# The fifth score products of two heads as 64-row products in opposite halves of the array, and score banks by head

## The chip, the core and the metric

The kernel runs as one program on one core of a Trainium2 chip. The metric is the device time of one execution in microseconds (us). The engines are named as in the profile: PE is the matrix engine (TensorE), PEld its weight loads, DVE is VectorE, ACT is ScalarE, POOL is GpSimd, SP is the engine that issues most of the DMAs. PSUM is the memory into which PE writes its sums; this kernel uses it in banks of 512 float32 values for each of 128 partitions.

## The reference

A trunk of two layers works on 256 positions of 2048 channels. Each layer normalises its input, projects it, sends one part through a causal convolution with layer norm and one part through latent attention with 16 heads, gates and adds both, projects the sum and adds it to the input. What the change touches are the scores of attention:

```python
q = jnp.concatenate([q[..., :QK_NOPE], rope(q[..., QK_NOPE:], cos, sin)], axis=-1)   # 128 + 64 values
k = jnp.concatenate([k[..., :QK_NOPE], rope(k[..., QK_NOPE:], cos, sin)], axis=-1)
...
s = jnp.einsum('bqhd,bkhd->bhqk', q_i, k, preferred_element_type=jnp.float32) * scale
mask = key_chunk[None, :] <= q_chunk[:, None]        # chunks of 64, blocks of 128 queries
p = jax.nn.softmax(jnp.where(mask, s, -jnp.inf), axis=-1)
```

So a head's query and key have 128 values without and 64 with rotation ("rotary"). The queries come in two blocks of 128. Block 0 sees the first 128 keys only, block 1 all 256.

## The kernel before

**Split numbers.** Every float32 operand of a product is split into a high part and a low part (a float32r value and the rest), and a product is formed as high·high + low·high + high·low. For the big projections ACT makes `hi` from the raw weights, DVE makes `lo`, and PE multiplies pieces of 2 × 128 rows of weights: 12 products of 512 columns for each piece, into the banks `acc`. The weights for `hi` are prepared three pieces ahead of PE, those for `lo` two.

**The order of the work.** A wrapper (`InOrder`, its recording line is L135, which is why every row of the profile names L135) keeps each engine's instructions in the order in which the code issues them. `background(n)`, called after each piece, advances a slot counter and issues the attention steps that fall due in that slot between the pieces of the projections; `late` steps come at the end of the same slot. For each pair of heads, eight pairs in a layer, the steps are: factors, scaling of keys, a turn through DRAM, splits, `scores` (17 slots after the pair's start, or up to 4 later), `maxima` right behind it, `exponentials` two slots later, and later the values.

**The operands of the scores.** `nope_t` holds the 128 plain values of the pair's queries and keys, high and low, with the 128 values on the array's rows. The 64 rotary values fill half of the rows: head 0 owns rows 0 to 63, head 1 rows 64 to 127 (`halves`). In `rope_t[:, 0, h]`, the rotary queries, the head's own half holds the high part and the other half the low part; in `rope_t[:, 1, h]`, the keys, both halves hold the high part. `rope_l[:, h]` has the keys' low part in the own half and zeros in the other.

**`scores` (L835).** For each head three products make the scores of block 0, with high·high and low·high in the one half of the columns and high·low in the other. Five products of 256 columns each make the scores of block 1; the fifth is the rotary queries against `rope_l`, where the zeros cancel the other half. The sums stand in two banks: `s0` has block 0 of both heads, `s1` block 1 of both heads. That is 16 products for a pair.

**`maxima` (L859).** ACT copies one half of block 0's columns from PSUM to `sx`, DVE adds the other half, overwrites the masked corners of `sx` and of `s1`, and takes the negated maxima into `nb`. `exponentials` (L873) then reads `sx` and `s1`. At the very end of the program `products_at_end` (L303) uses the bank of `s0` for one last quarter of the output.

Of the kernel before, what the change touches and what calls it, by code (L numbers as in the profile page):

```python
# [11 lines left out]
F32 = mybir.dt.float32  # L12
# [7 lines left out]
P = 128  # L20
T = 2
SEQ = 256
# [101 lines left out]
def trunk(ctx: ExitStack, tc: tile.TileContext, xT, x, g_in, pos, win, wuq, wukv, wpc, wpm, wo, cst, rows, invf, out):  # L124
# [19 lines left out]
    pe, vec, act, gps, sp = (InOrder(e) for e in (nc.tensor, nc.vector, nc.scalar, nc.gpsimd, nc.sync))  # L144
# [16 lines left out]
    s_p = pool("s", 1, space=PSUM)  # L161
# [140 lines left out]

    def products_at_end(last, n, pts, stat, evacuate, evacuate_half):  # L303

        own = s_p.tile([P, n // 2], F32, tag="s0", name="right_half")

        def issue(t, places, out, columns=slice(0, n), start=False, stop=False):
            todo = [(j, kk, p) for j in places for p in range(3) for kk in range(KS)]
            for at, (j, kk, p) in enumerate(todo):
                hi, lo, _ = done[last[j]]  # L310
                sh, sl = stat(NCT - KS * len(last) + j * KS + kk, t)
                stationary, w = ((sh, hi), (sl, hi), (sh, lo))[p]
                pe.matmul(out, stationary, w[:, kk, columns], start=start and at == 0, stop=stop and at == len(todo) - 1)

        half = n // 2
        issue(0, (0, 1), pts[0][:, :n], stop=True)
        evacuate(0, pts[0][:, :n])
        issue(1, (0,), pts[1][:, :n])
        issue(1, (1,), pts[1][:, :half], slice(0, half), stop=True)
        evacuate_half(0, pts[1][:, :half], True)  # L320
        evacuate_half(half, pts[1][:, half:n], False)
        issue(1, (1,), own, slice(half, n), start=True, stop=True)
        evacuate_half(half, own, True)

    def product(planned, stat, evacuate, evac_at=EVAC_AT, costs=(0.0, 0.0), before=None, tardy=None, final=None):
# [8 lines left out]
        for j, i in enumerate(mine):  # L334
            for a in range(HI_AHEAD + 1):
                split_hi(i + a)
                if a <= LO_AHEAD:
                    split_lo(i + a)
            hi, lo, _ = done[i]
            if before:  # L340
                before(j)
            if final and j >= len(mine) - 2:
                if j == len(mine) - 1:
                    products_at_end(mine[-2:], n, pts, stat, evacuate, final)
                background(n)
                continue
            for t, kk, part in order_of_products(i, j == len(mine) - 1, j == tardy):
                k = j * KS + kk
                sh, sl = stat(k, t)
                stationary, w = ((sh, hi), (sl, hi), (sh, lo))[part]  # L350
                pe.matmul(
                    pts[t][:, :n], stationary, w[:, kk, :],
                    start=k == 0 and part == 0, stop=k == nk - 1 and part == 2,
                )
            if j == len(mine) - 1:
                steps.insert(0, (clock[0] + 1 + evac_at, costs, evac))
            background(n)
# [205 lines left out]
    for l in range(DEPTH):  # L563
# [101 lines left out]
        def pair_of(b, A=A):  # L665
            if b not in A.pairs:


                A.pairs[b] = dict(
                    qk=work2.tile([P, T, 4, 6, 32], F32, tag="qk", name="qk"),  # L670
                    vh=A.v_split[b % 3][0],
                    vl=A.v_split[b % 3][1],
                    ss=small.tile([P, 2, T, 2], F32, tag="ss_p", name="ss_p"),
                )
            return A.pairs[b]
# [87 lines left out]
        def attention(b, pair_of=pair_of, ss_d=ss_d, kpe=kpe, ccq=ccq, ssq_t=ssq_t, gqk=gqk, A=A):  # L763
            p, st = pair_of(b), {}
            nope_t, rope_t, rope_k, rope_l = A.nope_t, A.rope_t, A.rope_k, A.rope_l
# [35 lines left out]
            halves = (slice(0, ROPE), slice(ROPE, 2 * ROPE))  # L801
# [31 lines left out]
                at_slot(1, lambda: [vec.tensor_sub(lo, z, hi.bitcast(F32)) for lo, z, hi in subs], 1.8)  # L833

            def scores():  # L835
                s0 = s_p.tile([P, 2, 2, P], F32, tag="s0", name="s0")
                s1 = s_p.tile([P, 2, SEQ], F32, tag="s1", name="s1")

                for h in range(2):
                    qs = slice(0, P)  # L840
                    pe.matmul(s0[:, h], rope_t[:, 0, h, qs], rope_k[:, :, h, qs], start=True, stop=False)
                    pe.matmul(s0[:, h, 0, :], nope_t[:, 1, h, qs], nope_t[:, 2, h, qs], start=False, stop=False)
                    pe.matmul(s0[:, h], nope_t[:, 0, h, qs], nope_t[:, 2:4, h, qs], start=False, stop=True)
                for h in range(2):
                    qs = slice(P, SEQ)
                    terms = [
                        (rope_t[:, 0, h, qs], rope_t[:, 1, h, :]),
                        (nope_t[:, 0, h, qs], nope_t[:, 2, h, :]),
                        (nope_t[:, 0, h, qs], nope_t[:, 3, h, :]),
                        (nope_t[:, 1, h, qs], nope_t[:, 2, h, :]),  # L850
                        (rope_t[:, 0, h, qs], rope_l[:, h, :]),
                    ]
                    for n, (qa, ka) in enumerate(terms):
                        pe.matmul(s1[:, h, :], qa, ka, start=n == 0, stop=n == len(terms) - 1)
                st["s"] = s0, s1

                late.append(maxima)
# [66 lines left out]
            later(NOPE_AT, split_nope, 0.0, 1.8)  # L924
            later(ROPE_AT, split_rope, 0.0, 2.5)
            later(SCORES_AT, scores, 1.85, 0.35)
            later(EXP_AT, exponentials, 0.0, 3.3)
            later(P_BACK_AT, lambda: back_in("p"))
# [7 lines left out]
        s1 = layer_c.tile([P, 2, SEQ], F32, tag="s1c", name="s1c")  # L936
# [508 lines left out]
```

## Time and profile before

| | |
|---|---|
| time, median of 3 runs | 1876.08 us (1876.0 to 1877.35) |
| profiled execution, first to last instruction | 1875.0 us on core 0, granted TensorE clock 1.000 |
| what lies around the span, by the median | 1.1 us (the profiled execution's time as a whole is not listed) |
| PE, matmuls | 1869.4 us busy, 8577 products |
| DVE, ACT, POOL busy | 84%, 73%, 26% |
| the chain that ended last | PE 99%: `acc` 96%, `s` 2%, `o_ps` 1% |
| score products `s<-qk_t` | 224 of 256 columns, 32 of 128 columns, all of 128*128 |

A product's row on PE gives its start and a modelled end; products are pipelined, so the next one starts before the last one's row ends. What a product costs in a busy stretch is the distance between two starts. In a shape such as "128*128 128x256" the first two numbers are the rows and columns of the weights, the last is the product's columns. Two layers with eight pairs each make 16 calls of `scores`.

### The profile page before, as it was taken

What the parts mean: (1) busy time and instruction counts of PE and PEld (TensorE: products, weight loads), DVE (VectorE), ACT (ScalarE), POOL (GpSimd) and SP (SyncE); (2) the same over time, 40 slices, a digit from 0 to 9 for tenths busy, and PEclk for the clock granted to TensorE, in tenths of its full rate; (3) what the DMA queues carried; (4) which work ended last, traced back from release to release, by engine and by line L of the source; (5) the groups of instructions that cost most, each with busy time, mean ns of one, the idle gap of its engine ahead of it and who ended that gap; (6) DMA issues with size and microseconds to landing.
All of it is one profiled execution on the core that took longest, in us unless ns stands there. A gap on an engine that the chain in (4) does not pass through costs nothing.

```text
span 1875.0 us, 27166 instructions
## 1 busy us (share of the span) xinstructions
PE 1869.4 (100%) x8577; PEld 1570.9 (84%) x8577; DVE 1578.0 (84%) x2453; ACT 1360.5 (73%) x2510; POOL 495.7 (26%) x942
## 2 busy tenths in 40 slices
PE   9999999999999999999999999999999999999999
PEld 8988888888888888888899888888888888888887
DVE  6899998898999988766679899889899999885664
ACT  7678888888888876644557688788889888574442
POOL 1055555542200000122221455555322000001210
PEclk9999999999999999999999999999999999999999
DMA  9688878787765566678876787887877556667775
GB/s 322 219 264 255 261 256 258 257 275 226 244 204 192 194 207 218 208 239 278 290 234 216 260 267 253 260 255 262 267 231 242 196 191 204 206 206 222 239 250 166
DMA packets 138960, 445.05 MB, mean 237 GB/s; under 512 B 23680, under 2 KB 29312, under 8 KB 138816
## 3 DMA queue, kind: packets, MB, share of 16 engines
q1 hardware_dynamic: 105120, 359.89, 59.2%
q0 software_dynamic: 32832, 82.62, 13.8%
q8 instruction: 67, 1.10, 0.2%
q10 hardware_dynamic: 864, 0.80, 0.1%
q14 instruction: 77, 0.63, 0.1%
HBM read 399.18 MB, written 44.04 MB: 236 GB/s over the span
## 4 chain that ended last, share of the span: by engine, by line
PE 99%; DMA 1%; DVE 0%; ACT 0%; SPq 0%; issue 0%; DVEq 0%
PE acc L135 96%; PE s L135 2%; PE o_ps L135 1%; DMA raw<-in_win 0%; DMA gx<-in_g 0%; DVE xres L135 0%; ACT hi L135 0%; PE var L135 0%; PE mu L135 0%; SPq L135 0%; DVEq L135 0%
## 5 line engine op out<-in xcount | busy, mean ns | idle before, releaser
L135 ACT CAST hi<-raw 128x1024 fp32r<-128x1024 f32 (+3 forms) x682 | 700.3, 1033 | 405.0 <-PE acc L135 348.9
L135 DVE TENSOR_TENSOR lo<-raw,hi 128x1024 fp32r<-128x1024 f32 (+3 forms) x682 | 814.0, 1195 | 191.5 <-PE acc L135 145.7
L135 PE MATMUL acc<-hi,hT 128*128 128x512 f32 (+2 forms) x1728 | 419.6, 382 | 0.0
L135 PEld LDWEIGHTS acc<-hi,hT 128*128 128x128 f32 x1728 | 319.6, 188 | 59.1
L135 PE MATMUL acc<-hi,h_hi 128*128 128x512 f32 (+2 forms) x864 | 260.5, 383 | 1.3 <-ACT hi L135 1.3
L135 PE MATMUL acc<-hi,h_lo 128*128 128x512 f32 (+2 forms) x864 | 260.1, 382 | 0.0
L135 ACT ACTIVATE tap<-u_t,cst 128x256 f32<-128x256 f32 x542 | 235.7, 501 | 2.8 <-DVE v_t L135 2.8
L135 PE MATMUL acc<-lo,h_hi 128*128 128x512 f32 (+2 forms) x864 | 229.7, 382 | 0.0
L135 PE MATMUL acc<-lo,hT 128*128 128x512 f32 (+2 forms) x864 | 229.3, 382 | 0.0
L135 DVE TENSOR_TENSOR v_t<-v_t,tap 128x512 f32<-128x512 f32 x271 | 186.4, 688 | 9.7 <-DVE v_t L135 0.9
L135 POOL DMA_DIRECT2D turned<-turn_d x88 | 49.4, 562 | 531.0 <-DVE v_t L135 315.0
L135 PEld LDWEIGHTS acc<-hi,h_lo 128*128 128x128 f32 x864 | 161.0, 188 | 30.1
L135 PEld LDWEIGHTS acc<-hi,h_hi 128*128 128x128 f32 x864 | 160.0, 188 | 30.9 <-ACT hi L135 2.2
L135 PEld LDWEIGHTS acc<-lo,h_hi 128*128 128x128 f32 x864 | 160.5, 188 | 30.2 <-DVE lo L135 0.3
L135 PEld LDWEIGHTS acc<-lo,hT 128*128 128x128 f32 x864 | 160.6, 188 | 29.9
L135 DVE SCALAR_TENSOR_TENSOR v_t<-u_t,cst,v_t 128x256 f32<-128x256 f32 x418 | 178.4, 480 | 2.0
L135 POOL DMA_DIRECT2D turn_d<-gate x184 | 100.5, 554 | 290.6 <-DVE gate L135 177.6
L135 PE MATMUL acc<-hi,ycT 128*128 128x512 f32 x512 | 127.8, 389 | 0.0
L135 PE MATMUL acc<-hi,oT 128*128 128x512 f32 x512 | 127.7, 389 | 0.0
L135 PE MATMUL acc<-hi,yT 128*128 128x512 f32 x512 | 127.5, 388 | 0.0
L135 PE MATMUL acc<-hi,qkc 128*128 128x512 f32 x448 | 115.4, 389 | 0.0
L135 PEld LDWEIGHTS acc<-hi,ycT 128*128 128x128 f32 x512 | 96.1, 188 | 20.0
(176 smaller groups left out, 2227.1 us busy)
## 6 DMA issues: line engine op xcount, KB each, us to landing
raw<-in_win SPq DMA_DIRECT2D x382, 512.0 KB, 4.2
raw<-in_wpm SPq DMA_DIRECT2D x64, 512.0 KB, 3.3
raw<-in_wpc SPq DMA_DIRECT2D x64, 512.0 KB, 4.2
raw<-in_wo SPq DMA_DIRECT2D x64, 512.0 KB, 4.9
raw<-in_wukv SPq DMA_DIRECT2D x32, 512.0 KB, 4.1
turned<-turn_d POOLq DMA_DIRECT2D x56, 256.0 KB, 4.7
raw<-in_win SPq DMA_DIRECT2D x32, 384.0 KB, 4.6
raw<-in_wuq SPq DMA_DIRECT2D x24, 512.0 KB, 4.3
```

What stands on the lines that cost most here:

```text
L135: ins = getattr(self.engine, name)(*a, **k)
```

## The change

The fifth product of each head now takes only the 64 rows of the head's own half, for the queries as weights and for the keys, in place of 128 rows of which 64 met zeros. The two fifth products stand next to each other behind the other fourteen. A pair's scores stay 2 banks, but each bank now holds one head (block 0 in its first 256 columns, block 1 in its last 256), and both banks are one tile, `s`. `products_at_end` takes the same tile and uses the first 256 columns of it.

```diff
         def products_at_end(last, n, pts, stat, evacuate, evacuate_half):
 
-        own = s_p.tile([P, n // 2], F32, tag="s0", name="right_half")
+        own = s_p.tile([P, 2, 512], F32, tag="s", name="right_half")[:, 0, : n // 2]
...
             def scores():
-                s0 = s_p.tile([P, 2, 2, P], F32, tag="s0", name="s0")
-                s1 = s_p.tile([P, 2, SEQ], F32, tag="s1", name="s1")
+                s = s_p.tile([P, 2, 512], F32, tag="s", name="s")
+                s0 = s[:, :, :SEQ].rearrange("p h (i k) -> p h i k", i=2)
+                s1 = s[:, :, SEQ:]
...
+                qs = slice(P, SEQ)
                 for h in range(2):
-                    qs = slice(P, SEQ)
                     terms = [
                         (rope_t[:, 0, h, qs], rope_t[:, 1, h, :]),
                         (nope_t[:, 0, h, qs], nope_t[:, 2, h, :]),
                         (nope_t[:, 0, h, qs], nope_t[:, 3, h, :]),
                         (nope_t[:, 1, h, qs], nope_t[:, 2, h, :]),
-                        (rope_t[:, 0, h, qs], rope_l[:, h, :]),
                     ]
                     for n, (qa, ka) in enumerate(terms):
-                        pe.matmul(s1[:, h, :], qa, ka, start=n == 0, stop=n == len(terms) - 1)
+                        pe.matmul(s1[:, h, :], qa, ka, start=n == 0, stop=False)
+                for h in range(2):
+                    own = halves[h]
+                    pe.matmul(s1[:, h, :], rope_t[own, 0, h, qs], rope_l[own, h, :], start=False, stop=True)
```

On PE, at the first pair of the first layer, the scores stood like this between two products of a projection (`acc64`; `qk_t0` is the tile that holds `nope_t`, `rope_t` and `rope_l`; what a row waits for is in brackets, and the shape is that of the output):

```order
L135 MATMUL acc64_1_1910<-lo68_1990,h_hi_151 128x512 x2
L135 MATMUL s0_2073<-qk_t0_1397 128x256 [waits DVE_49,Activation_49,Pool_49]
L135 MATMUL s0_2073<-qk_t0_1397 128x128
L135 MATMUL s0_2073<-qk_t0_1397 128x256
L135 MATMUL s0_2073<-qk_t0_1397 128x256 [waits DVE_49,Activation_49]
L135 MATMUL s0_2073<-qk_t0_1397 128x128
L135 MATMUL s0_2073<-qk_t0_1397 128x256
L135 MATMUL s1_2074<-qk_t0_1397 128x256 x10
L135 MATMUL acc64_0_1909<-hi69_1992,h_hi_151 128x512 [waits Activation_49]
```

At the same place of PE in the changed kernel, all sixteen write one tile:

```order
L135 MATMUL acc64_1_1910<-lo68_1990,h_hi_151 128x512 x2
L135 MATMUL s_2073<-qk_t0_1397 128x256 [waits DVE_49,Activation_49,Pool_49]
L135 MATMUL s_2073<-qk_t0_1397 128x128
L135 MATMUL s_2073<-qk_t0_1397 128x256
L135 MATMUL s_2073<-qk_t0_1397 128x256 [waits DVE_49,Activation_49]
L135 MATMUL s_2073<-qk_t0_1397 128x128
L135 MATMUL s_2073<-qk_t0_1397 128x256 x11
L135 MATMUL acc64_0_1909<-hi69_1992,h_hi_151 128x512 [waits Activation_49]
```

The number of products, their place and PE's own waits are the same; the last two of the x11 are the ones of 64 rows, which these rows do not tell since they give the output's shape.

On DVE, at `maxima` of the same pair, the rows before were these (`sx` and `nb` belong to `maxima`, `lo` is the next piece of weights):

```order
L135 TENSOR_TENSOR sx<-s_2073,sx 128x256 [waits Activation_49]
L135 MEMSET sx 64x2x64 [waits DVE_49]
L135 MEMSET s_2074 64x2x64 [waits PE_49]
L135 TENSOR_REDUCE nb<-sx 128x2 [waits DVE_49]
L135 TENSOR_REDUCE nb<-s_2074 128x2 [waits DVE_49]
L135 TENSOR_TENSOR nb<-nb,r_p 128x4 [waits DVE_49]
L135 TENSOR_TENSOR lo_2102<-raw_1915,hi_2057 128x1024 [waits DMAHW5_49]
```

In the changed kernel DVE has there:

```order
L135 TENSOR_TENSOR sx<-s,sx 128x256 [waits Activation_49]
L135 MEMSET sx 64x2x64 [waits DVE_49]
L135 MEMSET s 64x2x64
L135 TENSOR_REDUCE nb<-sx 128x2 [waits DVE_49]
L135 TENSOR_REDUCE nb<-s 128x2 [waits DVE_49]
L135 TENSOR_TENSOR nb<-nb,r_p 128x4 [waits DVE_49]
L135 TENSOR_TENSOR lo_2101<-raw_1915,hi_2057 128x1024 [waits DMAHW5_49]
```

The order is the same, but the memset of the scores no longer waits for PE by itself. ACT's copy, on which the first row waits, now waits for all sixteen products, since block 0 and block 1 share one tile; before, it waited for the six products of block 0 alone.

## The prediction

> **What bounds the kernel now.** I read the page's busy times first, then PE's waits, then the chain of waits around one call of `scores`.
>
> ```profile
> span 1875.0 us, 27166 instructions
> PE 1869.4 (100%) x8577; PEld 1570.9 (84%) x8577; DVE 1578.0 (84%) x2453; ACT 1360.5 (73%) x2510; POOL 495.7 (26%) x942
> PEclk9999999999999999999999999999999999999999
> ```
>
> PE is busy from end to end at a clock that never drops. That alone could be many products stretched by waits, so the list of PE's waits decides it (us in total, times, longest):
>
> ```profile
> PE acc L135 <- ACT hi L135: 1.3, 2, 0.9
> PE warm L135 <- PEq L1434: 0.8, 1, 0.8
> ```
>
> In the whole span PE waited 2.1 us for others. So the kernel ends when PE has issued its last product: a change moves the time by what it adds to or takes from PE's own sequence, unless it delays ACT or DVE so much that PE begins to wait for `hi` or `lo`. The chain of waits at the first pair shows the stretch that is changed (start, us, what):
>
> ```profile
> 175.95 0.91 PE acc L135 x4
> 176.85 1.89 PE s L135 x16
> 178.74 3.43 PE acc L135 x15
> ```
>
> Sixteen score products take 1.89 us, with projections tight on both sides. There are 16 such stretches, 30.2 us, and the change touches the last two products of each.
>
> **What the two fifth products cost today.** Their starts are read from PE's timeline in two narrow stretches (start, length, instructions merged):
>
> ```profile
> 178.34 0.40 PE L135 MATMUL s<-qk_t 128*128 128x256 f32 x2
> ...
> 178.46 0.28 PE L135 MATMUL s<-qk_t 128*128 128x256 f32 x1
> 178.58 0.40 PE L135 MATMUL acc<-hi,h_hi 128*128 128x512 f32 x1
> ```
>
> The last three starts are 178.34, 178.46 and 178.58, so a product of 256 columns costs 0.12 us, though its row lasts 0.28: 0.16 us of it, the tail, lies under the next product. A pair's two fifth products cost 0.24 us, all 32 of them 3.84 us. That is all the time the change works on.
>
> **What the two cost if they run at the same time.** Two products of 64 rows and 256 columns stream in the time of one at best, 0.12 us. Each still needs its own weight load. How closely loads follow each other is seen where PE restarts after its longest wait (PE above, its loads below):
>
> ```profile
> 12.19 0.73 PE L135 MATMUL acc<-hi,h_hi 128*128 128x512 f32 x2 [0.94 <-ACT hi L135]
> 12.76 0.62 PE L135 MATMUL acc<-hi,h_lo 128*128 128x512 f32 x2
> ...
> 12.19 0.30 PEld L135 LDWEIGHTS acc<-hi,h_hi 128*128 128x128 f32 x2 [1.36 <-ACT hi L135]
> 12.53 0.42 PEld L135 LDWEIGHTS acc<-hi,h_lo 128*128 128x128 f32 x2
> 13.00 0.19 PEld L135 LDWEIGHTS acc<-hi,h_hi 128*128 128x128 f32 x1
> ```
>
> One load lasts 0.19; two that follow at once take 0.30, so the second starts 0.11 after the first. The same 0.11 shows on PE: the first two products after the wait take 0.73, two in a running stream 0.62. A load that nothing hides costs 0.11 us. If the pair's loads queue behind one another, the pair costs 2 × 0.11 = 0.22 us and saves 0.02; if they too run side by side, it costs 0.12 and saves 0.12. Over 16 calls that is a gain of 0.3 to 1.9 us and no more.
>
> The Trainium skill states a price for such a pair in "TensorE: Matmul & The Clock Gate", Part 3 on packing small matmuls: products in different row groups together take one product's duration and about 4 ns for each further tile. By it the gain would be the upper one, 1.9 us; no run here has shown such a pair yet.
>
> **What the change of row count costs.** All 8577 products of this profile use weights of 128 rows. The changed kernel goes from 128 rows to 64 and back at each call, 32 switches in all. No row shows a switch. The nearest rows bound it:
>
> - From below, nothing: the stream passes from 512 columns to 256 to 128 and back inside the 1.89 us without a visible gap. That is a change of shape too, but one along time, not across the array's rows.
> - A switch that lets the array run empty costs at least the tail that is now covered, 0.28 − 0.12 = 0.16 us.
> - If the next weights may not be loaded before the array is empty either, their load stands exposed as at the restart: 0.16 + 0.11 = 0.27 us.
>
> With the tail alone, the loads of the pair being ready: 2 × 0.16 − 0.12 saved = +0.20 us a call, +3.2 us in 16 calls, 1879.3. With exposed loads at both switches, and the pair's second load 0.11 behind the first so that only 0.01 is saved: 2 × 0.27 − 0.01 = +0.53 a call, +8.5 us, 1884.6.
>
> I take it that the array does run empty at both switches. This is an assumption: the pair is to work as two separate halves, which no product of this profile does, so nothing shows that such products can be in flight together with one that uses all rows; the passage between column counts is no counterexample, since columns only follow one another. Between the two prices nothing in the trace chooses: loads do run one product ahead in the stream, but only for weights of the same rows. So I take the middle, +0.365 a call, 16 × 0.365 = +5.8 us: **1881.9 us** on the median of 1876.08 (span 1875.0, with 1.1 us around it, which the change does not touch).
>
> The Trainium skill speaks against the change here: "TensorEngine Tiling (Array Packing)", under Tiling Modes, Key Properties, says that changing the tiling mode, as against the tile, drains TensorE. It names no price, and no run here shows it so far.
>
> **What moves on ACT and DVE.** ACT's copy into `sx` waits for all sixteen products now. The timeline of that pair and the waits of ACT show what stands behind it:
>
> ```profile
> 177.58 0.37 ACT L135 COPY sx<-s 128x256 f32<-128x256 f32 x1 [1.01 <-PE s L135]
> 177.85 1.05 ACT L135 CAST hi<-raw 128x1024 fp32r<-128x1024 f32 x1
> 177.99 0.42 DVE L135 TENSOR_TENSOR sx<-s,sx 128x256 f32<-128x256 f32 x1 [1.33 <-ACT sx L135]
> 178.84 0.17 DVE L135 MEMSET s<- 64x128 f32 x1 [0.17 <-PE s L135]
> 179.98 1.22 DVE L135 TENSOR_TENSOR lo<-raw,hi 128x1024 fp32r<-128x1024 f32 x1
> 180.62 1.06 ACT L135 CAST hi<-raw 128x1024 fp32r<-128x1024 f32 x1 [0.32 <-PE acc L135]
> 182.99 0.50 ACT L135 ACTIVATE pr<-sx,nb,r_p 128x128 f32<-128x128 f32 x1
> 185.41 0.62 PE L135 MATMUL acc<-lo,h_hi 128*128 128x512 f32 x2
> ...
> ACT sx L135 <- PE s L135: 18.3, 10, 2.4
> ```
>
> The copy started at 177.58, and the last score product was visible to DVE's memset at 178.84, so the copy will wait some 1.2 us longer, and behind it on ACT the cast to `hi`, on DVE `sx`, the maxima and the `lo` of 179.98. In ten of the sixteen calls ACT waited for PE; in the other six it came so late that the products were nearly or wholly done. Cover: that `lo` was ready at 181.20, and counted in pieces of 12 products it is used at 185.41, 4.2 us later; `hi` is made one piece further ahead, and at 180.62 ACT had to wait for PE to free a buffer. The exponentials start at 182.99, 1.2 us later than the new end of the maxima (the `lo` behind them would start at 181.2). So I cost this at nothing. Without the cover it would be up to 10 × 1.2 = 12 us.
>
> **The rest, with one answer each.** The memset, the copy, the maxima and the exponentials read or write the same number of elements, now across two banks, and are off PE's path. `right_half` at the end takes a tile that was last read long before:
>
> ```profile
> L135 ACT ACTIVATE pr<-s,nb,r_p x32: 548/552/559, 184.0 to 1366.1; 128x256 f32<-128x256 f32 x32
> ```
>
> Its last reader started at 1366.1, so the last quarter waits for nothing new. No DMA is added or moved.
>
> **The rivals.**
>
> 1. *No stall, loads one after another.* A row switch costs what a column switch does, and the pair is bound by its loads: −0.3 us, 1875.8. For it: loads already run ahead in the stream, and column counts change freely. Against: halves and whole array would be at work in one pass, of which no row has an example. It decides if the first projection product after the pair starts no later than 0.24 us after the pair's first. This is the mechanism on the other side: not slower. Chance 0.22.
> 2. *No stall, products and loads side by side*, the full 0.12 a call: −1.9 us, 1874.2. The closest rows show loads 0.11 apart, which speaks against it. Chance 0.07. By the packing rule above this is what would happen if the switches were free.
> 3. *Nothing is gained or lost*: the pair runs one after the other, at 0.12 each, without stalls, so the change does not do what it says: 1876.1. Chance 0.06.
> 4. *A switch costs more than any row here*: at 0.5 us each, about twice my upper price, 2 × 0.5 − 0.12 = 0.88 a call, +14 us, 1890. Chance 0.09, since even a restart after a real wait shows no more than 0.27 beyond the wait.
> 5. *The late copy reaches PE*: `lo` comes after PE wants it in the ten calls, up to +12 us, 1888. It decides once the delay passes 4 us; it is 1.2. Chance 0.03.
>
> **How the numbers follow.** My forecast, a stall at both switches between 1879.3 and 1884.6, gets 0.52; what is left, 0.01, goes to a gain that nothing here prices. 0.2% of the time is 3.75 us, about what a measurement of this kernel can tell from no change: the bounds are 1872.3 and 1879.8. Of my forecast's 0.52 about 0.47 lies above 1879.8, where its lowest end falls just short. Slower: 0.47 + 0.09 + 0.03 = 0.59. Same: 0.05 + 0.22 + 0.07 + 0.06 = 0.40. Faster by more than 0.2% gets the remaining 0.01, since even PE's whole waiting of 2.1 us and the full 1.9 us would together only just pass it. The range takes in the forecast's both ends and rivals 1 and 3, with what the runs spread by themselves (1876.0 to 1877.35): 1875.3 to 1885.6. It leaves out rivals 2, 4 and 5 and the last 0.01, 0.20 in all. The forecast's own range is 1879.3 to 1884.6.
>
> **What the changed profile would show.** Right: the chain's stretch of `s` with sixteen products grows from 1.89 to between 2.09 and 2.42 us, all of it at the fifth products and the first `acc` product after them; PE's list of waits stays at two short rows, since no semaphore is involved; the row "ACT sx <- PE s" grows by some 10 × 1.2 to about 30 us. Wrong: the stretch is 1.87 us or less (rivals 1 and 2), or the two 64-row products stand 0.12 apart with 0.12 before and behind (rival 3), or a row "PE acc <- DVE lo" appears (rival 5).

## The result and the profile after

The changed kernel takes 1880.35 us (median of 11 runs, 1879.9 to 1880.77), before 1876.0 (11 runs, 1875.3 to 1877.35). The ratio is 1.0022, 95% interval 1.0014 to 1.0031: slower by 4.35 us. The interval lies above no change and has the prediction's bound of 0.2% inside it. The forecast was 1881.9.

The page and the list of PE's waits, after:

```profile
span 1878.6 us, 27166 instructions
PE 1874.1 (100%) x8577; PEld 1570.9 (84%) x8577; DVE 1577.1 (84%) x2453; ACT 1358.1 (72%) x2510; POOL 494.1 (26%) x942
...
PE warm L135 <- PEq L1437: 0.8, 1, 0.8
PE acc L135 <- ACT hi L135: 0.2, 1, 0.2
```

PE issues the same number of products and waits for others 1.0 us in all, less than before, and still its busy time is 4.7 us longer. So the time is inside PE's own sequence. The groups by shape show which products are new (count, then busy us and mean ns):

```profile
L135 PE MATMUL s<-qk_t 128*128 128x256 f32 x192 | 28.9, 290 | 0.0
L135 PE MATMUL s<-qk_t 128*128 128x128 f32 x32 | 7.1, 222 | 0.0
L135 PE MATMUL s<-qk_t 64*128 64x256 f32 x32 | 6.1, 379 | 0.0
```

There are 32 products of 64 rows, and one lasts 379 ns where one of 128 rows and 256 columns lasts 290. The chain of waits from one call of `scores` to the next shows where a call grows. First before:

```profile
247.14 1.89 PE s L135 x16
249.03 8.19 PE acc L135 x36
257.21 1.16 PE o_ps L135 x8
258.37 24.50 PE acc L135 x108
282.88 1.89 PE s L135 x16
```

Then after:

```profile
246.72 1.96 PE s L135 x16
248.67 8.39 PE acc L135 x36
257.06 1.16 PE o_ps L135 x8
258.22 24.50 PE acc L135 x108
282.72 1.96 PE s L135 x16
```

The 108 products in the fourth piece take the same 24.50 us. The scores take 0.07 more, and the projections right behind them 0.20 more (8.39 against 8.19), so a call costs 0.27 us more, three quarters of it booked on products that the change does not touch. In single starts (PE first, then its weight loads, each from a narrow stretch of the first call; the first row holds the last product of 128 rows and, merged into it, the pair):

```profile
177.25 0.59 PE L135 MATMUL s<-qk_t 128*128 128x256 f32 x3
...
177.46 0.38 PE L135 MATMUL s<-qk_t 64*128 64x256 f32 x2
177.77 0.50 PE L135 MATMUL acc<-hi,h_hi 128*128 128x512 f32 x1
...
177.13 0.19 PEld L135 LDWEIGHTS s<-qk_t 128*128 128x128 f32 x1
177.45 0.18 PEld L135 LDWEIGHTS s<-qk_t 64*128 64x128 f32 x2
177.77 0.30 PEld L135 LDWEIGHTS acc<-hi,h_hi 128*128 128x128 f32 x2
```

Read it in four steps. The last 128-row product starts at 177.25, and the pair not 0.12 later but 0.21, at 177.46: a stall of 0.09. The pair's loads start at 177.45, at the pair's own start, where a load in the running stream starts one product ahead (the load at 177.13 is for the product of 177.25): it stands exposed, and the pair's rows last 0.38 instead of 0.28, 0.10 more. Both products of the pair start at once, and so do both loads: two of them take 0.18 together, what one takes. Behind the pair the same again: the next product starts 0.31 after the pair, which is the pair's exposed load of 0.10, the usual 0.12 and once more a stall of 0.09; its load starts with it at 177.77, and it lasts 0.50 instead of 0.39, 0.11 more.

So a call pays 0.09 + 0.10 going in, 0.09 + 0.11 coming out, and saves 0.12: +0.27 us, in 16 calls +4.3 us, which is the difference of the medians. (The spans differ by 3.6 only: the wait for the first weights at the start happened to be 1.1 us shorter in this profile, 0.2 against 1.3 in the rows of PE's waits. The prediction's 1.1 us around the span set a median against one profile's span. The profiled execution of the changed kernel took 1880.34 us with a span of 1878.6, so 1.7 lay around it.)

### The profile page after: what moved, and what is told of

Same layout as the page of the kernel before. It is cut to its first block, busy times and chain, and to the rows that moved or that the text cites. A ratio compares the mean times of both kernels' runs of the same rounds, so it can differ in the third digit from the quotient of the medians.

```text
span 1878.6 us, 27166 instructions
## 1 busy us (share of the span) xinstructions
PE 1874.1 (100%) x8577; PEld 1570.9 (84%) x8577; DVE 1577.1 (84%) x2453; ACT 1358.1 (72%) x2510; POOL 494.1 (26%) x942
## 4 chain that ended last, share of the span: by engine, by line
PE 99%; DMA 0%; DVE 0%; ACT 0%; SPq 0%; issue 0%; DVEq 0%
PE acc L135 96%; PE s L135 2%; PE o_ps L135 1%; DMA raw<-in_win 0%; DMA gx<-in_g 0%; DVE xres L135 0%; ACT hi L135 0%; PE mu L135 0%; PE var L135 0%; SPq L135 0%; DVEq L135 0%
## 5 line engine op out<-in xcount | busy, mean ns | idle before, releaser
L135 PEld LDWEIGHTS acc<-hi,oT 128*128 128x128 f32 x512 | 96.1, 188 | 20.0
```

What stands on the lines that cost most here:

```text
L135: ins = getattr(self.engine, name)(*a, **k)
```

## The experiments

The theory: PE stalls at each change between 128 and 64 rows, as it would if the array had to run empty first, and the next weights are loaded only then. The rivals: the layout by head or the late copy costs the time (A), each 64-row product has a cost of its own (B), the stall belongs to a certain neighbour (C), a pair's loads queue (D). Each kernel is shown as its edit to the changed kernel. For each, the chain of waits gives one call of `scores` and the piece behind it, to be read against 1.89 and 8.19 before, 1.96 and 8.39 after.

**The layout, the order and the late copy without 64-row products.**

```diff
                 for h in range(2):
-                    own = halves[h]
-                    pe.matmul(s1[:, h, :], rope_t[own, 0, h, qs], rope_l[own, h, :], start=False, stop=True)
+                    pe.matmul(s1[:, h, :], rope_t[:, 0, h, qs], rope_l[:, h, :], start=False, stop=True)
```

> The new tile, the banks by head, the fifth products side by side in the order and ACT's later copy, but all products of 128 rows again. Theory (the array runs empty at each switch of the row count): no switch, so the time of before, 1876.0, and a stretch of sixteen score products of 1.89 us; the later copy costs nothing. Rival A (the layout by head or the later copy costs the time): 1880.3, as with the change.

Measured: 1876.1 us against 1875.7, ratio 1.0001 (0.9993 to 1.0010). The chain, and ACT's wait for the copy:

```profile
246.92 1.89 PE s L135 x16
248.80 8.19 PE acc L135 x36
...
ACT sx L135 <- PE s L135: 31.0, 12, 3.6
```

The stretches are those of before to the hundredth. ACT waits 31.0 us in 12 calls for the scores, where it was 18.3 in ten before, and none of it reaches PE. Rival A falls, and with it the prediction's fifth rival: the late copy is hidden.

**One 64-row product in place of two.** Head 0's fifth product keeps its 64 rows and stands last, head 1's gets 128 back.

```diff
-                for h in range(2):
-                    own = halves[h]
+                for h in (1, 0):
+                    own = halves[h] if h == 0 else slice(0, P)
```

> Only head 0's fifth product has 64 rows, and it stands last; head 1's, just ahead of it, has 128. Theory: two switches are left and nothing runs side by side, so the pair's saving of 0.12 us a call is gone: about 0.38 us a call, 6.1 us in 16 calls, 1882.1, slower than the change though fewer products have 64 rows. Rival B (each 64-row product has a cost of its own, half of the change's 4.35 us each): 1878.2. Rival A: 1880.3.

Measured: 1881.9 us, ratio 1.0034 (1.0021 to 1.0048). The chain:

```profile
246.63 2.07 PE s L135 x16
248.71 8.40 PE acc L135 x36
```

With half as many 64-row products the kernel is 6.2 us over before, where the change is 4.35 over it. Both switches are still there (8.40 behind the call, as with the change), and the call itself is 0.11 longer: the two products no longer share their time. That is the saving of a pair, seen by taking it away. Rival B wanted 1878.2 and falls.

**Both products of 64 rows, but apart.** Each stands behind the four others of its head.

```diff
                     for n, (qa, ka) in enumerate(terms):
                         pe.matmul(s1[:, h, :], qa, ka, start=n == 0, stop=False)
-                for h in range(2):
                     own = halves[h]
                     pe.matmul(s1[:, h, :], rope_t[own, 0, h, qs], rope_l[own, h, :], start=False, stop=True)
```

> Both fifth products have 64 rows, each right behind the other four of its head, so each stands alone between products of 128 rows. Theory: four switches a call and no saving, 2 x 0.38 = 0.77 us a call, 12.3 us, 1888.3. Rival B: the same two products, 1880.3. Rival A: 1880.3.

Measured: 1888.75 us, ratio 1.0069 (1.0055 to 1.0083): 13.05 us over before, 0.8 us a call, with the same 32 products of 64 rows as the change. The chain:

```profile
247.81 2.46 PE s L135 x16
250.27 8.43 PE acc L135 x36
```

The call takes 2.46, which is 0.57 over before, and the piece behind it 0.24. What counts is how often the row count changes, four times a call here, and not how many products have 64 rows.

**The pair first in the call.** It stands between a projection's product of 512 columns and block 1's other products; block 0 comes last.

```diff
+                qs = slice(P, SEQ)
+                for h in range(2):
+                    own = halves[h]
+                    pe.matmul(s1[:, h, :], rope_t[own, 0, h, qs], rope_l[own, h, :], start=True, stop=False)
...
-                        pe.matmul(s1[:, h, :], qa, ka, start=n == 0, stop=False)
+                        pe.matmul(s1[:, h, :], qa, ka, start=False, stop=n == len(terms) - 1)
```

> The pair of 64-row products stands first in the call, right behind a projection's product of 512 columns and ahead of the other score products; block 0 comes last. Theory: a switch waits for what is in flight whatever its size, and the next load stands exposed whatever it is for: 1880.3, as with the change. Rival C (the stall is a matter of the 512-column product behind the pair, or of the first and last product of a sum): under 1878.

Measured: 1880.85 us, ratio 1.0027 (1.0016 to 1.0038). The chain, and PE's starts at the pair:

```profile
246.80 2.16 PE s L135 x16
248.97 8.21 PE acc L135 x36
...
282.45 0.39 PE L135 MATMUL acc<-lo,h_hi 128*128 128x512 f32 x1
282.77 0.38 PE L135 MATMUL s<-qk_t 64*128 64x256 f32 x2
283.08 0.38 PE L135 MATMUL s<-qk_t 128*128 128x256 f32 x1
```

The whole 0.27 is now inside the call (2.16), and the piece behind it is back at 8.21. The pair starts 0.32 after the 512-column product where the next one would start after 0.23, again 0.09 late, and the 256-column product behind the pair lasts 0.38 instead of 0.28. So the price depends neither on which neighbour stands where, with 256 and 512 columns, nor on the pair's place in the sum; rival C falls. By the chain a call and the piece behind it cost 0.27 to 0.29 us more than before, some 4.5 us in 16 calls. The rest of the measured 5.15 lies outside the calls: the first score product starts anywhere between 175.4 and 176.7 us in the eight profiles, and the first experiment, whose calls are those of before, also came out 0.4 over it.

**Four pairs in one visit, and the same work with 128 rows.** Both add the low part of the rotary keys four times; the second uses 128 rows as in the first experiment.

```diff
-                for h in range(2):
-                    own = halves[h]
-                    pe.matmul(s1[:, h, :], rope_t[own, 0, h, qs], rope_l[own, h, :], start=False, stop=True)
+                for i in range(4):
+                    for h in range(2):
+                        own = halves[h]
+                        pe.matmul(s1[:, h, :], rope_t[own, 0, h, qs], rope_l[own, h, :], start=False, stop=i == 3)
```

> The pair of 64-row products is issued four times in a row at its place, so the low part of the rotary keys is added four times. It adds three pairs to each call and no switch. Theory with products and loads side by side: 0.12 us for a further pair, 3 x 0.12 x 16 = 5.8 us over the change, 1886.1. Rival D (the loads of a pair queue, 0.11 each): 0.22 for a further pair, 1890.9. Rival B (each 64-row product costs 0.25 in all): 24 us over the change, 1904.

> The same fourfold fifth products with the layout of the change, but of 128 rows each, so the low part of the rotary keys is added four times here too. Every theory: six further products a call of 0.12 us, 6 x 0.12 x 16 = 11.5 us over before, 1887.5. Against the run with four 64-row pairs it shows whether the switches are paid back: by the theory that one is 1.4 us faster, by rival D it is 3.4 us slower.

Measured on the same chip: with 64 rows 1885.84 us (1885.37 to 1886.43; ratio to before 1.0051, 1.0035 to 1.0068), with 128 rows 1887.40 (1886.87 to 1887.84; 1.0060, 1.0045 to 1.0075). The intervals of the ratios overlap; the four runs of each do not, and the chain shows the difference inside the call. Four pairs of 64 rows, and their loads:

```profile
248.11 2.31 PE s L135 x22
250.42 8.37 PE acc L135 x36
...
286.02 0.53 PEld L135 LDWEIGHTS s<-qk_t 64*128 64x128 f32 x8
...
286.48 0.28 PE L135 MATMUL s<-qk_t 64*128 64x256 f32 x2
286.69 0.50 PE L135 MATMUL acc<-hi,h_hi 128*128 128x512 f32 x1
```

Eight products of 128 rows in their place:

```profile
247.88 2.61 PE s L135 x22
250.49 8.19 PE acc L135 x36
```

Eight loads take 0.53 us: 0.18 for the last pair and 0.35 for the three steps before it, 0.12 a pair. So a further pair costs 0.12, as rival D's 0.22 would not allow. The last pair (286.48) has no exposed load, its rows last 0.28, and the next product starts 0.21 after it: the stall on the way out is 0.09 by itself too. With four pairs the 64-row form wins 0.30 in the call and loses 0.18 behind it: 0.12 us a call better by the chain, 1.6 us in the whole by the medians.

No experiment pointed to a version that beats both kernels. A visit to 64 rows costs 0.38 to 0.39 us and each pair in it saves 0.12. By these numbers it pays from the fourth pair on (no run has two or three), and a call of `scores` has one. Not tried was the pair with both heads in one bank, so whether the two halves need a bank each is not shown.

## Why the prediction was right

- **What bounds the kernel:** right. PE still waits for 1.0 us in the whole span (0.8 and 0.2), and what the change adds stands between PE's own starts.
- **A stall at both switches:** right: one stall goes with each change of row count (two, two, four and two of them in the changed kernel, with one product, apart, and first), and none appears between the two halves, which start within the hundredth. That the array is empty in a stall, as the prediction assumed, is not shown: no row tells it, and the next product starts 0.07 us before the modelled end of the row ahead of it. "TensorEngine Tiling (Array Packing)" of the Trainium skill, under Tiling Modes, Key Properties, draws the line at the same place: a change of the mode drains, a change of the tile does not. This trace agrees on where the stalls stand and adds the price, 0.09 plus an exposed load of 0.10 to 0.11 us.
- **The size of the stall:** the term was mis-sized in two parts that offset each other. The tail was taken as 0.16 us, the end of a product's row minus the next one's start; it measured 0.09, because PE goes on before the modelled end of a row. Whether loads are held at a switch was left open and met in the middle; they are held at both, so that part was near its upper bound.
- **The pair:** the upper price let its loads queue, 0.11 apart, and kept only 0.01 of the saving (0.02 by its own count of two loads of 0.11). They start together, and the whole 0.12 is saved. The packing rule of the Trainium skill in "TensorE: Matmul & The Clock Gate", Part 3, has it so (about 4 ns for a further tile), and this trace agrees, with both starts within the hundredth.
- **The number:** 0.19 + 0.20 − 0.12 = +0.27 a call, where the forecast had 0.365 between bounds of 0.20 and 0.53. That it came as near as it did is partly luck. The middle between the bounds had no reason of its own, and in it the two tails were 0.14 too dear, the loads 0.10 too cheap and the saving 0.055 too small.
- **The profile's sign:** the chain's stretch of sixteen products was to grow to 2.09 to 2.42 and grew to 1.96. The stretch ends with the row of the last score product, so it has the first switch less the saving (0.19 − 0.12), and the second switch stands in the row behind it; both rows together have the 0.27.
- **The other rivals:** the first three fall with the starts above: the first projection product comes 0.31 us after the pair's start, where rivals 1 to 3 allowed 0.24 at most. The fourth, 0.5 us a switch, is more than twice what was measured. (The 0.27 that the prediction sets against it from a restart is its own sum; of it the rows of the restart show the exposed load, 0.11.)
- **The late copy:** right. "ACT sx <- PE s" went to 33.2 us in 12 calls where about 30 was said, at no cost. (By the rows that the prediction shows, the exponentials of 182.99 stood 1.8 us behind 181.2, not 1.2, so the cover was larger than it says.) The changed kernel's rows:

```profile
177.88 0.37 ACT L135 COPY sx<-s 128x256 f32<-128x256 f32 x1 [2.53 <-PE s L135]
...
ACT sx L135 <- PE s L135: 33.2, 12, 3.8
```

## What to carry to other kernels

On a matrix engine that is busy from end to end, count changes of the row count, not products: here one visit to 64 rows cost 0.38 us, three times the 0.12 that a pair of 256-column products saves. At these prices half-height products pay only where four or more such pairs stand in a row. And look for the price of a new kind of instruction on its neighbours too: three quarters of this one were booked on the products behind the pair.

## What was not expected of the hardware

The weight loads of the two halves run side by side as the products do: two take 0.18 us together, and eight in pairs 0.53, where two loads of 128 rows in a row take 0.30. And the wait at a switch does not last until the modelled end of the product's row: after 256 columns the next product started 0.21 us after its forerunner's start (row 0.28), after 512 columns 0.32 (row 0.39).
